# Six pairs in seven products: buffers for turned blocks, issues held back for free buffers, and an order laid out with one server for all DMAs

## The chip, the cores and the metric

The kernel runs on one core of a Trainium2 chip. The time of a run is the device time in microseconds (us) of that core, for one execution of the whole program. The number compared is the median over runs. The core has five engines that run their own instruction streams in order: TensorE (PE), VectorE (DVE), ScalarE (ACT), GpSimd (POOL) and SyncE (SP), which here issues nearly all transfers. Transfers are carried out by 16 DMA engines.

## The reference

Two decoder layers work on 256 tokens of width 1024, all in float32. Each layer is a half-step feed-forward block (SwiGLU), a mixer, and a second half-step feed-forward block:

```python
def swiglu(h, w_gate, w_up, w_down):
    return (jax.nn.silu(h @ w_gate) * (h @ w_up)) @ w_down

for layer in range(2):
    x = x + 0.5 * swiglu(rms_norm(x, ffn1_norm[layer]), ffn1_w_gate[layer], ffn1_w_up[layer], ffn1_w_down[layer])
    h = rms_norm(x, mix_norm[layer])
    ...   # layer 0: mLSTM beside cross-attention to 256 memory tokens; layer 1: dilated attention beside it
    x = x + mix
    x = x + 0.5 * swiglu(rms_norm(x, ffn2_norm[layer]), ffn2_w_gate[layer], ffn2_w_up[layer], ffn2_w_down[layer])
    ...   # after layer 0: keys and values for layer 1 are projected from x
```

The hidden width of the feed-forward blocks is 2816. The four of them hold most of the work, and the change lies in them. They are called (layer, which) below: (0,1), (0,2), (1,1), (1,2).

## The kernel before

**Products.** A float32 number is split into a rounded part `hi` (a cast on ACT) and a remainder `lo` (a subtraction on DVE), both in the fast format fp32r, and a product takes three matmuls: hi by lo, hi by hi, lo by hi (`mm3`). Weights come from HBM as tiles `raw` of 128x1024 (half a megabyte) through a ring of six buffers and are split into a ring of eight `hi`/`lo` pairs. So each weight tile is one transfer, one ACT operation, one DVE operation, and then 12 or 24 matmuls of 512 columns for the two tiles of 128 tokens.

**A feed-forward stage.** The hidden width is cut into 11 blocks of 256. For a block `b`, step `gb` (function `gu`) makes gate and up products in one bank of PSUM, `gups`, 24 matmuls for each of the two token tiles; step `db` (function `dn`) multiplies the activated block by its rows of the down weights into the accumulators `acc`, 12 matmuls per token tile. Between them stands the activation: ACT computes `sil`, DVE multiplies it to `h`, which frees the PSUM bank, and the block has to be turned, so that the hidden width lies on the partitions. Turning goes over DRAM: DVE writes both tiles' 32x32 transposes into a buffer `hb` (`hidden_blocks`, L1056), SP writes it out (`hd<-hb`) and reads it back in another order (`ht<-hd`), and ACT and DVE split the result into `hhb` and `hlb` for the down products (`placed`, L1066).

**Pairs in seven products.** Some neighbouring blocks are done as a pair with seven products in place of eight, after Strassen and Winograd: step `25` is product 2 of the pair that begins at block 5, 12 matmuls. Stages (0,1) and (1,1) have one pair (blocks 5 and 6), (0,2) and (1,2) have two (5 and 6, 7 and 8). For a pair the weights are four quarters in parts `pa`, `pb`, `pc`. Sums of them are made partly by transfers that add to what is in the buffer (issued by POOL, `accum_op`), partly by DVE (`remade`). A pair needs 14 `lo` operations and 6 such sums on DVE.

**What sets the order.** The order of the steps of a stage is written out by hand in the table `PLANS` (L49). `p` in it prepares weights of the next mixer. Everything beside the matmuls (splits, activations, turning, transfers) is emitted by chains of small steps. While the kernel is built, a planner (`_Model`, L251) keeps a clock for each engine and the time at which each buffer becomes ready or free by its cost table; at each point the chain that is ready first is emitted next (`until`). Since every engine runs its stream in order, the planner's numbers decide what stands behind what on the chip. A transfer is charged to SP's clock at 360 bytes per ns and lands 2.0 us after that; an adding transfer costs twice as much and lands 3.0 us after. `part_ready` (L605) decides from SP's clock when the next part of a pair may be loaded. All vector, scalar and transfer instructions are recorded by one helper and so bear one line, L369; all matmuls are L787, transposes on PE L794.

**Buffers on the way of a turned block.** There are two `hb`, four slots `hd` in DRAM and one `ht`. A chain takes its buffer, and emits the instruction that fills it, as soon as its turn comes, whether or not the planner thinks that the buffer is free by then:

```python
blocks[b] = fp.tile([P, 4, 2, 2, 32], F32, tag="hb", bufs=2 if pairs else 1, name="hb")
...
d = self.dram.tile([P, 512], F32, tag="hd", bufs=4, name="hd")
...
ht = fp.tile([P, 4, P], F32, tag="ht", bufs=1, name="ht")
```

On the chip the instruction then waits at the head of its engine's queue until the buffer's last reader is done.

Of the kernel before, what the change touches and what calls it, by code (L numbers as in the profile page):

```python
# [40 lines left out]
def turned(layer, which, b):  # L41
# [24 lines left out]
SOON = 8  # L66
TWICE = ((0, 1), (0, 2), (1, 2))
# [183 lines left out]
class _Model:  # L251
# [10 lines left out]
    def __init__(self):  # L262
        self.clock = {"scalar": 0.6, "vector": 0.6, "gpsimd": 0.6, "tensor": 0.6, "sync": 1.6}
        self.marks = {}
        self.slots = {}
        self.banks = set()
        self.table = None
        self.latest = 0.0
        self.window, self.columns, self.fast = 0, 0.0, False
# [79 lines left out]
    def adding(self, cost, outs, ins):  # L349

        start = max([self.clock["sync"]] + [self.ready(a, True, "sync") for a in outs])
        self.clock["sync"] += cost
        end = start + cost + 3.0
# [5 lines left out]
class _Engine:  # L359
# [5 lines left out]
    def __getattr__(self, method):  # L365
        call, model, name = getattr(self.engine, method), self.model, self.name

        def traced(out, *args, **kw):
# [8 lines left out]
            if name == "sync" or name == "gpsimd" and method == "dma_start":  # L377
                cost = max(n * out.partition_size() * 4 / 360e3, 0.06)
                if kw.get("accum_op") is None:
                    model.run("sync", cost, outs, ins, 2.0)  # L380
                else:
                    model.adding(2 * cost, outs, ins)
# [51 lines left out]
class _Kernel:  # L434
# [138 lines left out]

    def leave(self, pool, n=1):
# [30 lines left out]
    def part_ready(self):  # L605
# [9 lines left out]
        if not all(c is not None and c.done for c in chains):  # L615
            return False
        return self.index[("st",) + self.pairs[p] + (m, k)] <= self.next + SOON or \
            self.model.clock["sync"] < self.now + LEAD
# [395 lines left out]
    def ffn_in(self, layer, which, after, memory, fp):  # L1014
# [7 lines left out]
        pending = set()  # L1022
# [33 lines left out]
        def hidden_blocks(b, t):  # L1056
            def steps(ps):
                h = self.work.tile([P, FB], F32, tag="ta", bufs=4, name="h")
                yield from activated(ps, t, h)
                if b not in blocks:  # L1060
                    blocks[b] = fp.tile([P, 4, 2, 2, 32], F32, tag="hb", bufs=2 if pairs else 1, name="hb")
# [4 lines left out]
        def placed(b, before):  # L1066
            yield from self.wait(*before)
            hb = blocks.pop(b)
            d = self.dram.tile([P, 512], F32, tag="hd", bufs=4, name="hd")
            nc.sync.dma_start(d, hb.rearrange("p j c t e -> p (j c t e)"))  # L1070
            yield
            ht = fp.tile([P, 4, P], F32, tag="ht", bufs=1, name="ht")
# [6 lines left out]
                                  ht.rearrange("p i (c e) -> p i c e", c=4))  # L1079
            for t in range(2):  # L1080
# [943 lines left out]
```

## Time and profile before

| what | value |
|---|---|
| median of 3 runs | 1009.35 us (1008.54 to 1010.49) |
| the profiled execution's own time | 1005.82 us |
| span in its trace, from the first to the last instruction | 1003.9 us |
| mean granted clock of TensorE | 0.991 |
| HBM read, written | 206.28 MB, 17.85 MB |
| queue of SP's transfers | 81816 packets, 60.3% of the DMA engines' span |
| queue of POOL's transfers, the adding ones | 3456 packets, 7.0% |

The trace is of one execution, and its instructions are named by line, engine, operation and tile. A row of the chain of waits gives a start, a length, and what stood there on the path that ended last. A row by stage gives the busy time of each engine in a window. A row of waits gives who waited, for whom, the sum, the count and the longest, in us. The stages of the program in this execution, read from the tile names, lie at: (0,1) from 25 to 202 us, the first mixer with the memory's projections to 321, (0,2) to 513, keys and values for layer 1 to 545, (1,1) to 743, the second mixer to 815, (1,2) to the end. "hi", "lo", "h", "hhb" and the like are the tiles above; an arrow points from what is read to what is written, from right to left.

### The profile page before, as it was taken

What the parts mean: (1) busy time and instruction counts of PE and PEld (TensorE: products, weight loads), DVE (VectorE), ACT (ScalarE), POOL (GpSimd) and SP (SyncE); (2) the same over time, 40 slices, a digit from 0 to 9 for tenths busy, and PEclk for the clock granted to TensorE, in tenths of its full rate; (3) what the DMA queues carried; (4) which work ended last, traced back from release to release, by engine and by line L of the source; (5) the groups of instructions that cost most, each with busy time, mean ns of one, the idle gap of its engine ahead of it and who ended that gap; (6) DMA issues with size and microseconds to landing.
All of it is one profiled execution on the core that took longest, in us unless ns stands there. A gap on an engine that the chain in (4) does not pass through costs nothing.

```text
span 1003.9 us, 13192 instructions
## 1 busy us (share of the span) xinstructions
PE 974.9 (97%) x4607; PEld 804.8 (80%) x4607; DVE 773.3 (77%) x1133; ACT 591.1 (59%) x935; POOL 72.1 (7%) x102
## 2 busy tenths in 40 slices
PE   9999999999999999989999999899999999899998
PEld 7777888899898878868778888788887788787777
DVE  6979876669976789879576787987566878896972
ACT  7776555577755565555476565656565674564641
POOL 0031000010010010000012001100011000100000
PEclk9999999999999999989999999999999999999999
DMA  9899688555455769854655799378457265998271
GB/s 361 330 316 299 240 274 341 169 171 194 137 167 191 237 186 297 300 136 170 228 190 169 264 312 306 84 257 280 162 202 288 112 229 191 259 293 255 73 251 42
DMA packets 85481, 224.99 MB, mean 224 GB/s; under 512 B 8172, under 2 KB 29608, under 8 KB 85416
## 3 DMA queue, kind: packets, MB, share of 16 engines
q1 hardware_dynamic: 81816, 211.54, 60.3%
q0 software_dynamic: 3456, 12.58, 7.0%
q8 instruction: 36, 0.59, 0.2%
q14 instruction: 29, 0.24, 0.1%
q10 hardware_dynamic: 144, 0.04, 0.0%
HBM read 206.28 MB, written 17.85 MB: 223 GB/s over the span
## 4 chain that ended last, share of the span: by engine, by line
PE 61%; DMA 16%; DVE 13%; issue 5%; ACT 4%; POOL 1%; SPq 1%; DVEq 0%; ACTq 0%; POOLq 0%
PE gups L787 25%; PE acc L787 17%; PE aps L787 6%; DVE lo L369 6%; DMA ht<-hd 5%; DMA hd<-hb 5%; PE oacc L787 4%; PE kvps L787 3%; DMA pb<-in_wts 2%; DMA raw<-in_wts 2%; ACT hi L369 2%; PE bqps L787 2%; PE tps L794 1%; DVE h L369 1%; DVE hb L369 1%
## 5 line engine op out<-in xcount | busy, mean ns | idle before, releaser
L369 DVE TENSOR_TENSOR lo<-raw,hi 128x1024 fp32r<-128x1024 f32 (+2 forms) x239 | 271.9, 1159 | 58.6 <-ACT hi L369 56.9
L369 ACT CAST hi<-raw 128x1024 fp32r<-128x1024 f32 (+2 forms) x239 | 233.0, 1003 | 66.6 <-DMA raw<-in_wts 26.2
L787 PE MATMUL gups<-lo,xh 128*128 128x512 f32 x552 | 214.2, 391 | 0.0
L787 PE MATMUL gups<-hi,xh 128*128 128x512 f32 x552 | 214.1, 390 | 0.0
L787 PE MATMUL gups<-hi,xl 128*128 128x512 f32 x552 | 214.0, 390 | 0.0
L787 PE MATMUL acc<-lo,hhb 128*128 128x512 f32 x304 | 120.4, 396 | 2.9 <-ACT hhb L369 2.2
L787 PEld LDWEIGHTS gups<-hi,xh 128*128 128x128 f32 x552 | 103.8, 188 | 22.1 <-ACT hi L369 0.8
L787 PEld LDWEIGHTS gups<-hi,xl 128*128 128x128 f32 x552 | 103.9, 188 | 21.7
L787 PEld LDWEIGHTS gups<-lo,xh 128*128 128x128 f32 x552 | 104.0, 188 | 21.4
L787 PE MATMUL acc<-hi,hlb 128*128 128x512 f32 x304 | 119.3, 393 | 0.0
L787 PE MATMUL acc<-hi,hhb 128*128 128x512 f32 x304 | 118.9, 391 | 0.0
L369 DVE SCALAR_TENSOR_TENSOR lo<-raw,gains,hi 128x512 fp32r<-128x512 f32 x128 | 88.9, 745 | 12.3 <-ACT hi L369 12.1
L369 ACT ACTIVATE hi<-raw,gains 128x512 fp32r<-128x512 f32 x128 | 84.0, 717 | 12.4 <-PE acc L787 4.6
L369 ACT ACTIVATE sil<-gups,rstd 128x256 f32<-128x256 f32 x76 | 35.9, 472 | 69.2 <-PE gups L787 56.0
L787 PEld LDWEIGHTS acc<-lo,hhb 128*128 128x128 f32 x304 | 57.5, 189 | 15.5 <-ACT hhb L369 3.1
L787 PEld LDWEIGHTS acc<-hi,hlb 128*128 128x128 f32 x304 | 57.3, 189 | 12.9 <-DVE hlb L369 0.9
L787 PEld LDWEIGHTS acc<-hi,hhb 128*128 128x128 f32 x304 | 57.4, 189 | 11.4
L787 PE MATMUL gups<-lo,th 128*128 128x512 f32 x128 | 52.9, 413 | 12.5 <-DVE h L369 12.2
L369 ACT CAST hhb<-ht 128x512 fp32r<-128x512 f32 x38 | 23.6, 621 | 69.2 <-DMA ht<-hd 69.2
L369 DVE SCALAR_TENSOR_TENSOR h<-gups,rstd,sil 128x256 f32<-128x256 f32 x76 | 36.3, 478 | 26.6 <-ACT sil L369 26.5
L369 ACT CAST hi<-pb 128x1024 fp32r<-128x1024 f32 x36 | 37.4, 1050 | 26.9 <-DMA pb<-in_wts 19.6
L787 PE MATMUL gups<-hi,th 128*128 128x512 f32 x128 | 51.8, 405 | 0.0
(231 smaller groups left out, 1592.9 us busy)
## 6 DMA issues: line engine op xcount, KB each, us to landing
raw<-in_wts SPq DMA_DIRECT2D x262, 512.0 KB, 5.3
raw<-in_wts SPq DMA_DIRECT2D x32, 384.0 KB, 3.6
hd<-hb SPq DMA_DIRECT2D x38, 256.0 KB, 5.4
ht<-hd SPq DMA_DIRECT2D x38, 256.0 KB, 4.2
pa<-in_wts SPq DMA_DIRECT2D x12, 512.0 KB, 6.7
pb<-in_wts SPq DMA_DIRECT2D x12, 512.0 KB, 4.5
pc<-in_wts SPq DMA_DIRECT2D x12, 512.0 KB, 6.4
pc<-in_wts POOLq DMA_DIRECT2D x12, 512.0 KB, 8.6
```

The lines of the kernel that those rows point to most:

```text
L369: call(out, *args, **kw)
L787: self.pe.matmul(out, lhsT=lhsT, rhs=rhs, start=start, stop=stop, skip_group_check=more)
L794: self.pe.transpose(out, in_, ident)
```

## The change

Four things change, and no instruction is added or taken away on any engine: the same operations stand in another order, with other buffers.

1. Buffers: three `hb` in place of two, two `ht` in place of one, eight slots `hd` in place of four.
2. A chain that needs an `hb` or an `ht` first waits, in the planner's time, until the oldest buffer is free (`vacant`), and no more blocks may be under way than there are buffers (`held_by`). Only then it takes the buffer and emits the instruction.
3. The planner's cost of transfers. One clock, `wire`, stands for all DMA engines together: each transfer, whoever issues it, begins when the one before it is through, takes a time from its size and the length of its contiguous pieces, 2.06 times as much if it adds, and lands 1.03 us later. The issuing engine's own clock is charged 0.34 us (0.9 for an adding transfer), and it waits there for the transfer's inputs and its buffer. `part_ready` goes by `wire`.
4. `PLANS` has a new order for all four stages. In (0,2) and (1,2) `d0` and `d1` stand further ahead, `d3` before `75`, and `d4` before `77`; in (1,1) the memory's step (tied to `g4`) before `g3`, `25` and `55` ahead of `d2`, `d3` and `d7` earlier; in (0,1) a `p` moves from behind `15` to before `35`.

```diff
 PLANS = {
-    (0, 1): "g0 g1 g2 g4 p d0 g3 25 55 d1 d2 45 d4 35 "
-            "d3 p 15 p 65 75 g7 p g8 d6 g9 p d5 d7",
-    (0, 2): "g0 g1 g2 g3 25 55 d0 d1 d2 45 35 15 65 75 "
-            "d3 g9 g4 27 57 d5 47 37 17 67 77 d4 d9 d6",
-    (1, 1): "g0 g1 g2 d0 g3 d1 g4 d2 25 55 45 "
-            "35 d3 15 65 d4 75 g7 g8 d5 d6 g9 d7",
-    (1, 2): "g0 g1 g2 g3 25 55 d0 d1 d2 45 35 15 65 75 "
-            "d3 g9 g4 27 57 d5 47 37 17 67 77 d4 d9 d6",
+    (0, 1): "g0 g1 g2 g4 p d0 g3 25 55 d1 d2 45 d4 p "
+            "35 d3 p 15 65 75 g7 p g8 d6 g9 p d5 d7",
+    (0, 2): "g0 g2 g1 d0 g3 d1 25 55 d2 45 35 15 65 d3 "
+            "75 g9 g4 27 57 47 d5 37 17 67 d4 77 d9 d6",
+    (1, 1): "g0 g1 g2 d0 g4 g3 d1 25 55 d2 45 "
+            "d3 35 15 65 d4 75 g7 g8 d5 d7 d6 g9",
+    (1, 2): "g0 g1 g2 d0 d1 g3 25 55 d2 45 35 15 65 d3 "
+            "75 g9 g4 27 57 d5 47 37 17 67 d4 77 d9 d6",
 }
...
+HB, HT = 3, 2
...
-    def adding(self, cost, outs, ins):
-        start = max([self.clock["sync"]] + [self.ready(a, True, "sync") for a in outs])
-        self.clock["sync"] += cost
-        end = start + cost + 3.0
+    def transfer(self, engine, outs, ins, adding=False):
+        size = outs[0].free_size() * outs[0].partition_size()
+        piece = min(self.piece(outs[0]), self.piece(ins[0]), 1024)
+        cost = size / piece * (8.2 + 0.147 * piece) / 16e3
+        at = max([self.ready(a, False, "sync") for a in ins] +
+                 [self.ready(a, True, "sync") for a in outs] + [self.clock[engine]])
+        self.clock[engine] = at + (0.9 if adding else 0.34)
+        begin = max(self.wire, at + 0.3)
+        if adding:
+            cost *= 2.06
+        self.wire = begin + cost
+        end = max(begin, at + 1.9 if adding else 0.0) + cost + 1.03
...
-                cost = max(n * out.partition_size() * 4 / 360e3, 0.06)
-                if kw.get("accum_op") is None:
-                    model.run("sync", cost, outs, ins, 2.0)
-                else:
-                    model.adding(2 * cost, outs, ins)
+                model.transfer(name, outs, ins, kw.get("accum_op") is not None)
...
+    def vacant(self, pool, tag, bufs):
+        waited = 0.0
+        while True:
+            t = self.model.free((id(pool), tag), bufs)
+            if t <= max(self.now, waited):
+                return
+            waited = t
+            self.model.latest = max(self.model.latest, t)
+            yield
...
-            self.model.clock["sync"] < self.now + LEAD
+            self.model.wire < self.now + LEAD
...
+        def held_by(count, most):
+            while count[0] >= most:
+                yield 0.05
+            count[0] += 1
...
                 if b not in blocks:
-                    blocks[b] = fp.tile([P, 4, 2, 2, 32], F32, tag="hb", bufs=2 if pairs else 1, name="hb")
+                    yield from self.vacant(fp, "hb", HB)
+                    yield from held_by(turning, HB)
+                    blocks[b] = fp.tile([P, 4, 2, 2, 32], F32, tag="hb", bufs=HB, name="hb")
...
-            d = self.dram.tile([P, 512], F32, tag="hd", bufs=4, name="hd")
+            d = self.dram.tile([P, 512], F32, tag="hd", bufs=8, name="hd")
             nc.sync.dma_start(d, hb.rearrange("p j c t e -> p (j c t e)"))
+            turning[0] -= 1
             yield
-            ht = fp.tile([P, 4, P], F32, tag="ht", bufs=1, name="ht")
+            yield from self.vacant(fp, "ht", HT)
+            yield from held_by(placing, HT)
+            ht = fp.tile([P, 4, P], F32, tag="ht", bufs=HT, name="ht")
```

**How instructions move.** SP's queue in (0,2), between the two pairs: the weights `raw189` to `raw191` belong to steps `g9` and `g4`, `hd` and `ht` are the way of a turned block. Before:

```order
L369 DMA hd_4145<-hb_4089 128x512
L369 DMA hd_4168<-hb_4065 128x512
L369 DMA raw189_4177<-in_wts 128x1024
L369 DMA raw190_4189<-in_wts 128x1024
L369 DMA raw191_4201<-in_wts 128x1024
L369 DMA ht_4235<-hd_4145 128x4x128
L369 DMA ht_4240<-hd_4168 128x4x128
L369 DMA hd_4264<-hb_4220 128x512
L369 DMA ht_4321<-hd_4264 128x4x128
```

The same place after the change:

```order
L389 DMA hd_4143<-hb_4070 128x512
L389 DMA pc2_4157<-in_wts 128x1024
L389 DMA raw186_4164<-in_wts 128x1024
L389 DMA raw187_4167<-in_wts 128x1024
L389 DMA raw190_4192<-in_wts 128x1024
L389 DMA hd_4198<-hb_4057 128x512
L389 DMA raw191_4201<-in_wts 128x1024
L389 DMA ht_4223<-hd_4143 128x4x128
L389 DMA hd_4273<-hb_4226 128x512
L389 DMA ht_4299<-hd_4198 128x4x128
L389 DMA raw192_4337<-in_wts 128x1024
L389 DMA ht_4351<-hd_4273 128x4x128
```

The two writes and the two reads of a pair's blocks stood in twos, and now stand apart: the second read is behind the write of a third block, `hd_4273`.

DVE at the same place. `hlb` splits a turned block, `h` frees the PSUM bank of a product, `lo` splits weights. Before:

```order
L369 TENSOR_TENSOR pa2_3971<-pa2_3971,pb2_3990 128x1024
L369 TENSOR_TENSOR hlb_4286<-ht_4235,hhb_4285 128x4x4x32
L369 SCALAR_TENSOR_TENSOR h_4293<-gups_4245,rstd_3292,sil_4294 128x256
L369 TENSOR_TENSOR hlb_4308<-ht_4240,hhb_4307 128x4x4x32
L369 STREAM_TRANSPOSE hb_4326<-h_4293 128x2x4x32
L369 TENSOR_TENSOR lo176_4315<-raw176_4133,hi176_4314 128x1024
L369 TENSOR_TENSOR lo177_4324<-raw177_4136,hi177_4323 128x1024
L369 SCALAR_TENSOR_TENSOR h_4343<-gups_4296,rstd_3357,sil_4344 128x256
```

And after, where the last `hb` of the third block and an `h` and `hb` of the fourth stand just ahead of the first row:

```order
L389 TENSOR_TENSOR lo176_4307<-pc0_4072,hi176_4306 128x1024
L389 TENSOR_TENSOR lo177_4317<-pc2_4157,hi177_4316 128x1024
L389 TENSOR_TENSOR hlb_4320<-ht_4223,hhb_4319 128x4x4x32
L389 TENSOR_TENSOR lo178_4330<-raw178_4130,hi178_4329 128x1024
L389 TENSOR_TENSOR pc0_4072<-pc0_4072,pa0_3958 128x1024
L389 SCALAR_TENSOR_TENSOR h_4339<-gups_4291,rstd_3357,sil_4340 128x256
L389 TENSOR_TENSOR lo179_4360<-raw179_4136,hi179_4359 128x1024
L389 TENSOR_TENSOR lo180_4363<-pb0_4014,hi180_4362 128x1024
L389 TENSOR_TENSOR pb0_4014<-pb0_4014,pa0_3958 128x1024
L389 STREAM_TRANSPOSE hb_4301<-h_4339 128x2x4x32
L389 TENSOR_TENSOR pc2_4157<-pc2_4157,pa2_3960 128x1024
L389 TENSOR_TENSOR hlb_4384<-ht_4299,hhb_4383 128x4x4x32
```

Two `hlb` with one `h` between them have become two `hlb` with eight other operations between them.

DVE in (1,1), at the memory's keys `kn` (two chains of scaling, `hss` and scaling again, each behind ACT's squares `sq`). Before:

```order
L369 TENSOR_TENSOR hlb_5975<-ht_5888,hhb_5974 128x4x4x32
L369 TENSOR_TENSOR lo248_5995<-pa_5626,hi248_5994 128x1024
L369 TENSOR_TENSOR lo249_5998<-pa_5628,hi249_5997 128x1024
L369 TENSOR_SCALAR kn_6016<-mkvps_5951,memr0_90 128x256
L369 TENSOR_TENSOR lo250_6008<-pb0_5759,hi250_6007 128x1024
L369 TENSOR_TENSOR pa_5626<-pa_5626,pb0_5759 128x1024
L369 TENSOR_REDUCE hss_6032<-sq_6018 128x4
L369 TENSOR_SCALAR kn_6044<-mkvps_5977,memr1_91 128x256
L369 TENSOR_TENSOR hlb_6042<-ht_6014,hhb_6041 128x4x4x32
L369 TENSOR_REDUCE hss_6066<-sq_6046 128x4
```

After:

```order
L389 TENSOR_SCALAR kn_5891<-mkvps_5813,memr0_90 128x256
L389 TENSOR_TENSOR lo244_5880<-raw244_5785,hi244_5879 128x1024
L389 TENSOR_REDUCE hss_5908<-sq_5893 128x4
L389 TENSOR_SCALAR kn_5918<-mkvps_5842,memr1_91 128x256
L389 TENSOR_REDUCE hss_5938<-sq_5920 128x4
L389 TENSOR_TENSOR lo245_5927<-raw245_5799,hi245_5926 128x1024
L389 TENSOR_TENSOR lo246_5933<-pa_5594,hi246_5932 128x1024
L389 TENSOR_TENSOR lo247_5951<-pa_5596,hi247_5950 128x1024
L389 TENSOR_TENSOR kn_5891<-kn_5891,rp_r_5911 128x256
L389 TENSOR_TENSOR kn_5918<-kn_5918,rp_r_5941 128x256
```

The `hlb` of a turned block no longer stands inside the two chains, and the pair's parts (`pa`) come after them.

More of the change, by code (lines that the diff above doesn't have):

```diff
@@ L262, in __init__ @@
     def __init__(self):
-        self.clock = {"scalar": 0.6, "vector": 0.6, "gpsimd": 0.6, "tensor": 0.6, "sync": 1.6}
+        self.clock = {"scalar": 0.6, "vector": 0.6, "gpsimd": 0.6, "tensor": 0.6, "sync": 2.1}
         self.marks = {}
@@ L267, in __init__ @@
         self.table = None
-        self.latest = 0.0
+        self.latest, self.wire = 0.0, 0.0
         self.window, self.columns, self.fast = 0, 0.0, False
@@ L347, in run, with piece @@
         self.latest = max(self.latest, end)
-    def adding(self, cost, outs, ins):
-        start = max([self.clock["sync"]] + [self.ready(a, True, "sync") for a in outs])
-        self.clock["sync"] += cost
-        end = start + cost + 3.0
+    @staticmethod
+    def piece(ap):
+        run = 1
+        for step, n in reversed(ap.ap[1:]):
+            if step != run:
+                break
+            run *= n
+        return run
+    def transfer(self, engine, outs, ins, adding=False):
[10 more added lines that the diff above has]
+        end = max(begin, at + 1.9 if adding else 0.0) + cost + 1.03
+        for a in ins:
+            self.mark(a, end, False, "sync")
         for a in outs:
@@ L1021, in ffn_in @@
         pairs = (layer, which) in PLANS
-        pending = set()
+        pending, turning, placing = set(), [0], [0]
+        def held_by(count, most):
+            while count[0] >= most:
+                yield 0.05
+            count[0] += 1
         def room(*key):
@@ L1079, in placed @@
                                   ht.rearrange("p i (c e) -> p i c e", c=4))
+            placing[0] -= 1
             for t in range(2):
```

## The prediction

> **What bounds the kernel now.** I read the page first, then the busy time by stage, then who made TensorE (PE) wait in each stage, and the chain of waits for what a wait costs afterwards.
>
> ```profile
> PE 974.9 (97%) x4607; PEld 804.8 (80%) x4607; DVE 773.3 (77%) x1133; ACT 591.1 (59%) x935; POOL 72.1 (7%) x102
> ```
>
> PE is the bound: 97% busy, and the program holds the same instructions before and after. So the change can win only what PE loses to waits. The stages (window, its length, then busy time and instructions of PE, its weight loads, VectorE (DVE), ScalarE (ACT) and GpSimd (POOL), the granted clock, the share of the DMA engines, GB/s):
>
> ```profile
> 202.00:321.00 119.00, 117.66 (x702) 107.49 (x702) 93.49 (x192) 78.17 (x158) 11.18 (x24) 1.00 0.52 170
> 321.00:513.00 192.00, 183.34 (x795) 149.31 (x794) 151.51 (x190) 106.71 (x147) 9.10 (x13) 0.97 0.67 216
> ...
> 545.00:743.00 198.00, 195.14 (x863) 161.16 (x862) 151.66 (x218) 118.62 (x181) 8.64 (x10) 0.99 0.70 226
> 743.00:815.00 72.00, 69.38 (x442) 53.90 (x441) 51.27 (x106) 42.79 (x96) 9.69 (x12) 1.00 0.57 211
> 815.00:1003.90 188.90, 178.96 (x788) 146.32 (x785) 144.96 (x180) 96.31 (x126) 7.90 (x10) 0.99 0.64 201
> ...
> 25.00:202.00 177.00, 174.68 (x787) 143.62 (x786) 141.96 (x182) 108.99 (x157) 14.03 (x15) 1.00 0.82 282
> ```
>
> The losses sit in three feed-forward stages: 192 − 183.3 = 8.7 us in (0,2), 9.9 us in (1,2) (some 3 of it the tail after the last product), 2.9 us in (1,1). Only these stages show a clock under 1.00. Who PE waited for, in (0,2), then (1,1), then (1,2):
>
> ```profile
> PE gups L787 <- DVE h L369: 5.9, 2, 4.6
> PE acc L787 <- ACT hhb L369: 1.8, 1, 1.8
> PE acc L787 <- DVE lo L369: 0.7, 1, 0.7
> ...
> PE tpk L794 <- DVE kn L369: 2.9, 1, 2.9
> ...
> PE gups L787 <- DVE h L369: 6.4, 3, 3.2
> PE acc L787 <- ACT hhb L369: 0.4, 1, 0.4
> ```
>
> And what followed these waits, from the chain (start, length, what, count):
>
> ```profile
> 438.72 5.44 PE gups L787 x12
> ...
> 449.63 10.89 PE gups L787 x48
> ...
> 489.43 2.51 PE acc L787 x6
> ...
> 636.76 9.07 PE gups L787 x36
> ...
> 865.64 3.04 PE gups L787 x12
> ...
> 931.97 4.61 PE gups L787 x12
> ```
>
> 48 matmuls in 10.89 us are 0.227 us each, 12 are 2.72. The 12 behind the 4.6 us wait took 5.44: half clock, 2.7 us more. By the same count the other rows lost 1.2, 0.9, 0.3 and 1.9 us. The Trainium skill ("TensorE: Matmul & The Clock Gate", section "HAM oscillation") puts the danger at PE gaps over about 3.4 us; the trace differs, since a gap of 1.8 us was followed by half clock and one of 3.2 by hardly any. By that rule only the first clock loss would be there, and the prizes below would be 4.3 us smaller; the sum goes by the rows.
>
> So the prizes are: **A** (0,2), start of the second pair, 4.6 + 2.7 = 7.3. **B** (0,2), end, 1.8 + 1.2 = 3.0. **C** (0,2), start of the first pair, (5.9 − 4.6) + 0.7 = 2.0. **D** (1,1), 2.9 + 0.9 = 3.8. **E** (1,2), first pair, 3.2 + 0.3 = 3.5. **F** (1,2), second pair, (6.4 − 3.2) + 1.9 = 5.1. Together 24.7 us: the most that can be won here.
>
> **Part by part.** *Two `ht` buffers and held-back issues.* Around A:
>
> ```profile
> 420.56 9.16 SPq L369 DMA_DIRECT2D ht<-hd  x2
> ...
> 434.31 0.62 ACT L369 CAST hhb<-ht 128x512 fp32r<-128x512 f32 x1 [7.54 <-DMA ht<-hd]
> ...
> 434.96 0.69 DVE L369 TENSOR_TENSOR hlb<-ht,hhb 128x512 fp32r<-128x512 f32 x1 [5.25 <-ACT hhb L369]
> ...
> 438.18 0.48 DVE L369 SCALAR_TENSOR_TENSOR h<-gups,rstd,sil 128x256 f32<-128x256 f32 x1
> ...
> 429.35 4.94 DMA ht<-hd
> ...
> L369 DVE TENSOR_TENSOR lo<-raw,hi 128x1024 fp32r<-128x1024 f32 x196 | 234.1, 1216 | 52.3 <-ACT hi L369 50.8
> ```
>
> Both reads are next to each other on SP's queue, but the second leaves only at 429.35, when `hlb` of the first has emptied the one buffer. DVE, in order, stands 5.25 us at the second `hlb`; behind it is the `h` that frees PE's bank. With a second buffer the read no longer waits for that `hlb`. In the new order it stands behind the write of a third block (`hd_4273` in the rows shown with the change), but after that block's last `hb` DVE has eight operations of 128x1024, one `hlb` and four small ones, 8 x 1.22 + 0.69 + 4 x 0.48 or about 12 us, before the second `hlb`, more than twice what the read took (4.94). Bounds for A: all 7.3 gone, or nothing (if adds delay the read). I take 5.3 of A and of F, the same place one layer later, 3.6 of 5.1, leaving a wait under 2 us at each.
>
> *B and the end of (1,2)* have the same serial pair of reads:
>
> ```profile
> 473.14 7.14 DMA ht<-hd
> ...
> 481.68 4.47 DMA ht<-hd
> ```
>
> The second could land some 5 us earlier. But the plan also moves `d4` in front of `77`: between product 7 of blocks 7 and 8 and the first down product of block 7 stand three groups of 24 matmuls (`d9 d6` and half of `g10`) instead of four, 16.3 us instead of 21.8. Gain and loss nearly cancel. For B I take 1.5 won (bounds 3.0 won, 3.0 lost); at the end of (1,2), **G**, where PE now waits 0.4 us, 1.5 lost (0 to 5).
>
> *C and E*: `d0` and `d1` now stand before `25`. In (0,2) `d1` (24 matmuls, 5.4 us) separates the last `g3` product from `25`, so the `h` that frees the bank and the `lo` have that much more time than the waits of 1.3 and 0.7. In (1,2) `g3` still touches `25`, but `d0 d1` in front leave DVE work done sooner. I take 1.5 of C's 2.0 and 2.0 of E's 3.5 (bounds: all, none).
>
> *D*: the memory's products move up (`g4` before `g3`).
>
> ```profile
> 615.63 9.27 DMA hd<-hb
> ...
> 627.90 0.62 ACT L369 CAST hhb<-ht 128x512 fp32r<-128x512 f32 x1 [5.12 <-DMA ht<-hd]
> ...
> 629.30 0.48 DVE L369 TENSOR_SCALAR kn<-mkvps,memr 128x256 f32<-128x256 f32 x1 [3.40 <-ACT sq L369]
> ```
>
> ACT stood 5.12 us at `hhb`, with the `sq` behind it for which DVE's `kn`, and then PE, waited. In the new order no `hlb` stands between the two `kn` chains. I take 3.3 of 3.8.
>
> *The other tight places*, **H**: `d1` of (0,2) and of (1,2) follow their block's last product by 72 matmuls (16.3 us), `d9` of (1,1) by 60 (13.6 instead of 19.1).
>
> ```profile
> 697.51 10.88 PE gups L787 x48
> ...
> 720.62 0.62 ACT L369 CAST hhb<-ht 128x512 fp32r<-128x512 f32 x1 [0.84 <-DMA ht<-hd]
> ```
>
> Block 9's products ended at 708.4; its `hhb` was ready 12.8 us later, 0.8 inside the new room. I take 1.0 lost (0 to 6). **J**: the new DMA times shift rows in the mixers too, whose stages idle 1.3 and 2.6 us, and in (0,1), 2.3: 1.0 lost (3 either way). The third `hb` buffer, the eight `hd` slots and the 0.3 to 0.4 us that a further SP issue takes add no instruction; costed at nothing, hidden under PE.
>
> **The sum:** 5.3 + 1.5 + 1.5 + 3.3 + 2.0 + 3.6 = 17.2 won, 1.5 + 1.0 + 1.0 = 3.5 lost: 13.7. The profiled execution took 1005.8 us (1003.9 of span, the end of the last window above, and 1.9 around it), so 992.1; it was 3.5 below the median of the timed runs, 1009.35. On that scale the forecast is **995.5 us**.
>
> **Rivals.** *1, the adds share the wire.* The planner now serves all transfers one after another. But in the window 866.5 to 878.2, with four adds under way (software queue q0, SP's queue q1):
>
> ```profile
> q0 software_dynamic: 405, 1.46, 65.1%
> q1 hardware_dynamic: 513, 1.64, 38.9%
> ...
> hd<-hb SPq DMA_DIRECT2D x1, 256.0 KB, 11.6
> ht<-hd SPq DMA_DIRECT2D x1, 256.0 KB, 6.2
> ```
>
> Both queues moved at once, and a turned block needed 11.6 + 6.2 = 17.8 us. In both (x,2) stages the block turned beside the first pair's adds now has less DVE work between its last `hb` and its `hlb`: in (0,2) ten operations of 128x1024 and two of half that size instead of nineteen and one; in (1,2) fewer still. 10 x 1.22 and, at half the time, 2 x 0.6 are 13.4 us: DVE would stand 4.4. A pair is 14 `lo` and 6 sums, 24.4 us of DVE against 84 matmuls, 19.1 of PE, so nothing there catches it up. Twice 4.4 lost on top of the forecast: 1004. The Trainium skill ("DMA: Bandwidth & Descriptors", section "Queues, rings and completion order") says that each DMA engine goes round its queues packet by packet, which these two rows agree with; by that rule this rival is the likelier the more adds are under way. Against it: the planner also counts an add dear, so it may place `hlb` late enough.
>
> *2, slower: the rooms of 16.3 us are too short.* At the end of (1,2):
>
> ```profile
> 963.93 0.42 SPq L369 DMA_DIRECT2D hd<-hb  x1
> ...
> 959.85 6.04 DMA hd<-hb
> ...
> 965.90 6.84 DMA ht<-hd
> ```
>
> The last product ended near 955.6 (13.6 us after 942.0), the write of block 7 left 8.3 us later; with 6.0 and 6.8 for the trips and 0.6 for `hhb` that is 21.7, 5.4 over the room, and with half clock after it some 7.5 a place. At three of the five places with 13.6 to 16.3 us that is 22.5, against 16.2 won elsewhere (13.7 plus the 2.5 of G and H): 1015.7. It decides once the trip exceeds 16.3 us at three places. Against it: `ht` took 2.9 there as the second read, and d0 and d1 start with quieter queues.
>
> *3, the stops only move.* DVE has no reserve inside a pair, and the new order's hold-ups fall elsewhere in the same runs: of the 17.2 us 3 to 7 stay won, less 3.5: about 1007.
>
> **How the numbers follow.** Forecast 0.58, rival 1 0.18, rival 2 0.11, rival 3 0.13. A measurement here tells 0.2%, 2 us, from no change. Faster: all of the forecast's case, 0.16 of rival 1, 0.07 of rival 3: 0.81. Same: 0.02 and 0.04: 0.06. Slower: rival 2 and 0.02 of rival 3: 0.13. The range runs from 984 (all 24.7 us won) to 1010, which takes in rivals 1 and 3; the forecast's own is 988 to 1002.
>
> **What would show it.** Right: the waits of PE for `h` in (0,2) and (1,2) fall from 12.3 us together to under 5, the wait for `kn` in (1,1) is gone, the clock in (0,2) is 0.99 or more, and no second read waits over 2 us for an `hlb`. Rival 1: DVE stands over 3 us at an `hlb` inside a first pair. Rival 2: PE waits for `hhb` at the ends of stages grow from 2.2 us to over 8. The forecast is wrong if PE idle in the three stages together stays over 17 us, or if the mixers' idle grows by more than 3.

## The result, and the profile after

The change made the kernel slower: 1024.39 us median of 4 runs (1022.39 to 1027.61) against 1008.94 us before, a ratio of 1.0153 with a 95% interval of 1.0123 to 1.0184. The forecast was 995.5 us, and the range ended at 1010. The profiled execution took 1022.39 us, with a span of 1020.7 and a mean granted clock of 0.985.

The page of the changed kernel, engines first:

```profile
PE 978.6 (96%) x4607; PEld 806.7 (79%) x4607; DVE 773.6 (76%) x1133; ACT 590.5 (58%) x935; POOL 70.3 (7%) x102
```

The work is what it was; DVE is busy 0.3 us longer and ACT 0.6 us shorter. PE is busy 3.7 us longer, with a granted clock of 0.985 against 0.991, and idle 13 us longer. Where, by stage (window, its length, then busy time and instructions of PE, its weight loads, DVE, ACT and POOL, the granted clock, the share of the DMA engines, GB/s), with every stage reaching to the first matmul of the next. The changed kernel:

```profile
0.00:204.40 204.40, 198.08 (x861) 160.52 (x862) 156.35 (x209) 126.26 (x192) 12.56 (x23) 0.98 0.82 284
204.40:323.90 119.50, 119.50 (x724) 109.44 (x722) 95.32 (x195) 80.16 (x164) 10.59 (x25) 1.00 0.53 176
323.90:517.50 193.60, 182.28 (x787) 147.95 (x785) 149.87 (x189) 104.75 (x144) 8.82 (x12) 0.96 0.66 212
...
553.80:754.50 200.70, 193.02 (x846) 157.59 (x845) 148.71 (x213) 114.52 (x175) 8.41 (x10) 0.99 0.68 222
754.50:830.60 76.10, 70.18 (x450) 55.05 (x448) 52.40 (x108) 43.84 (x97) 11.41 (x12) 1.00 0.53 193
830.60:1020.70 190.10, 179.23 (x784) 147.26 (x782) 143.94 (x180) 96.17 (x126) 7.92 (x10) 0.98 0.63 202
```

The same cut of the kernel before:

```profile
0.00:200.00 200.00, 196.44 (x862) 159.20 (x863) 155.50 (x209) 125.92 (x192) 15.96 (x23) 1.00 0.83 291
200.00:321.40 121.40, 120.06 (x723) 109.83 (x722) 95.55 (x195) 80.57 (x164) 11.55 (x25) 1.00 0.53 172
321.40:512.10 190.70, 182.04 (x788) 148.25 (x787) 150.38 (x189) 105.41 (x145) 8.85 (x12) 0.97 0.67 216
...
548.30:742.30 194.00, 191.14 (x845) 157.94 (x844) 147.86 (x213) 114.64 (x174) 8.64 (x10) 0.99 0.70 229
742.30:815.40 73.10, 70.48 (x448) 54.73 (x448) 52.37 (x108) 43.89 (x97) 9.69 (x12) 1.00 0.57 210
815.40:1003.90 188.50, 178.56 (x785) 146.00 (x783) 144.57 (x180) 95.91 (x126) 7.90 (x10) 0.99 0.63 201
```

(0,1) is 4.4 us longer, the first mixer 1.9 shorter, (0,2) 2.9 longer, (1,1) 6.7, the second mixer 3.0, (1,2) 1.6; with 0.1 for the keys and values that is the 16.8 us between the spans. No stage that was to gain gained. Who PE waited for in the changed kernel:

```profile
PE gups L814 <- DVE h L389: 17.0, 5, 6.9
PE tph L821 <- DVE h L389: 4.5, 3, 3.3
PE tpq L821 <- DVE qn L389: 3.3, 1, 3.3
PE mkvps L814 <- DVE h L389: 3.0, 2, 1.8
...
PE gups L814 <- DVE lo L389: 1.9, 1, 1.9
PE acc L814 <- ACT hhb L389: 1.4, 1, 1.4
```

The waits of `gups` for `h` in (0,2) and (1,2), which were to fall from 12.3 us together to under 5, are 14.8 there (7.2 and 7.6), and 17.0 in all; the longest is the one of place A, 6.9 where it was 4.6. PE's idle time in the three stages that were to gain is 29.9 us together; over 17 was the prediction's sign of being wrong. Two stops are new, of 3.3 us each: `h` at 22 us, in a stretch of (0,1) whose order was not changed, and `qn` in the second mixer.

**Place A.** DVE and ACT at the start of the second pair of (0,2):

```profile
437.11 1.23 DVE L389 TENSOR_TENSOR lo<-pc,hi 128x1024 fp32r<-128x1024 f32 x1 [2.24 <-ACT hi L389]
442.47 0.69 DVE L389 TENSOR_TENSOR hlb<-ht,hhb 128x512 fp32r<-128x512 f32 x1 [4.14 <-ACT hhb L389]
```

```profile
441.82 0.62 ACT L389 CAST hhb<-ht 128x512 fp32r<-128x512 f32 x1 [4.75 <-DMA ht<-hd]
```

DVE stands again, but at the first `hlb` of the place, not the second. The buffer is free; the read is late. What the DMA engines did around it, between 417 and 442 us (GB/s in 40 slices, then packets, MB and the share of the engines of each queue; q0 is that of the adds):

```profile
GB/s 210 243 177 262 236 282 308 269 367 390 380 403 433 410 429 419 426 413 423 403 393 419 403 322 284 220 213 200 211 249 239 232 252 232 229 211 215 204 178 59
...
q1 hardware_dynamic: 2555, 5.28, 56.7%
q0 software_dynamic: 576, 2.10, 43.4%
```

And what was issued from 413 to 427 us (count, size, median us from issue to landing):

```profile
raw<-in_wts SPq DMA_DIRECT2D x8, 512.0 KB, 9.3
...
pc<-in_wts SPq DMA_DIRECT2D x1, 512.0 KB
ht<-hd SPq DMA_DIRECT2D x1, 256.0 KB, 15.2
```

The two queues together fill all engines (56.7% and 43.4%). Nine weight transfers were issued in the 13 us ahead of the read, 9.3 us each in the median from issue to landing, so the later ones were still under way when it was issued; and three adds were issued behind it, from 428.27 to 431.64 us (a row of SP's queue, then two of POOL's):

```profile
426.57 0.38 SPq L389 DMA_DIRECT2D ht<-hd  x1
...
428.27 0.86 POOL L389 DMA_DIRECT2D pc<-in_wts  x1 [12.71 <-DMA pc<-in_wts]
...
431.64 0.86 POOL L389 DMA_DIRECT2D pb<-in_wts  x1 [1.62 <-issue]
```

The read lands 15.2 us after its issue. A read that has the wire to itself, in the same execution at 342 us, takes 2.6:

```profile
ht<-hd SPq DMA_DIRECT2D x1, 256.0 KB, 2.6
```

The same kind of window before the change (420 to 434 us), where the prediction's 4.94 us for the read came from, has a wire that lies idle for some 4 us, from 424 to 428:

```profile
GB/s 386 410 433 457 386 410 394 332 331 192 95 38 16 22 20 0 0 0 0 0 0 0 0 0 152 70 47 140 140 222 187 187 199 181 287 332 299 238 231 263
```

SP issued no weight transfer between 418 and 437 us. The read itself, from 429.35 us on, was not alone: two adds, issued at 426.98 and 429.25, ran beside it. So 4.94 us is the time of a read beside adds with no weights in its own queue.

**The second mixer.** ACT in the changed kernel, and below it in the kernel before:

```profile
785.84 1.05 ACT L389 CAST hi<-raw 128x1024 fp32r<-128x1024 f32 x1 [2.89 <-DMA raw<-in_wts]
786.80 0.55 ACT L389 ACTIVATE mp<-ms,nm,rqb 128x256 f32<-128x256 f32 x1
```

```profile
771.76 0.56 ACT L369 ACTIVATE mp<-ms,nm,rqb 128x256 f32<-128x256 f32 x1 [0.95 <-DVE nm L369]
...
773.81 1.06 ACT L369 CAST hi<-raw 128x1024 fp32r<-128x1024 f32 x1 [0.48 <-DMA raw<-in_wts]
```

A cast of weights has moved ahead of `mp`, and stands 2.9 us for its transfer; `qn`, for which PE waits, comes behind it. At 22 us it is a cast too, but not the wait of a single one. ACT in the changed kernel, and below it in the kernel before:

```profile
18.99 1.05 ACT L389 CAST hi<-raw 128x1024 fp32r<-128x1024 f32 x1 [2.04 <-DMA raw<-in_wts]
...
21.62 1.05 ACT L389 CAST hi<-raw 128x1024 fp32r<-128x1024 f32 x1 [0.31 <-DMA raw<-in_wts]
```

```profile
18.58 1.05 ACT L369 CAST hi<-raw 128x1024 fp32r<-128x1024 f32 x1 [2.03 <-DMA raw<-in_wts]
```

The stop of 2.0 us stands in both. The changed kernel has one cast more, the one at 21.62, ahead of the work that leads to `h`, which begins at 25.53 us and not at 23.78; and PE comes to the transpose of `h` sooner, its last product ahead of it beginning at 22.41 us and not at 24.26.

### The profile page after: what moved, and what is told of

Read it like the earlier page. It is cut to its first block, busy times and chain, and to the rows that moved or that the text cites. A ratio compares the mean times of both kernels' runs of the same rounds, so it can differ in the third digit from the quotient of the medians.

```text
span 1020.7 us, 13205 instructions
## 1 busy us (share of the span) xinstructions
PE 978.6 (96%) x4607; PEld 806.7 (79%) x4607; DVE 773.6 (76%) x1133; ACT 590.5 (58%) x935; POOL 70.3 (7%) x102
## 3 DMA queue, kind: packets, MB, share of 16 engines
q0 software_dynamic: 3456, 12.58, 6.6%
## 5 line engine op out<-in xcount | busy, mean ns | idle before, releaser
L814 PE MATMUL gups<-lo,xh 128*128 128x512 f32 x552 | 216.9, 396 | 4.3 <-DVE h L389 2.4
L389 DVE TENSOR_TENSOR hlb<-ht,hhb 128x512 fp32r<-128x512 f32 x38 | 26.1, 687 | 55.4 <-ACT hhb L389 55.4
```

The source lines that it names most:

```text
L389: call(out, *args, **kw)
L814: self.pe.matmul(out, lhsT=lhsT, rhs=rhs, start=start, stop=stop, skip_group_check=more)
```

## The experiments

All kernels ran beside the kernel before on the same chip. There are 4 to 10 runs of each. Runs of one kernel scatter by up to 1.6% (the kernel before: 1003.88 to 1008.96 in 13 runs on one chip, 996.53 to 1012.54 in 15 on another), so the ratios to before are compared, with 95% intervals:

| kernel | orders | planner's costs | median us | ratio to before |
|---|---|---|---|---|
| the change | new | new | 1024.39 | 1.0153 (1.0123 to 1.0184) |
| buffers_only (no issues held back) | old | old | 993.67 | 0.9873 (0.9838 to 0.9907) |
| held_back | old | old | 994.31 | 0.9899 (0.9830 to 0.9969) |
| old_costs | new | old | 1014.02 | 1.0081 (1.0052 to 1.0109) |
| old_plans | old | new | 1019.47 | 1.0126 (1.0083 to 1.0170) |
| late_landing | new | new, later landing | 1007.40 | 1.0010 (0.9994 to 1.0027) |
| late_old_plans | old | new, later landing | 997.70 | 0.9913 (0.9883 to 0.9942) |
| plain_adds | new | new; adds only copy | 1005.92 | 1.0005 (0.9978 to 1.0033) |
| plans_plain | new | old; adds only copy | 993.54 | 0.9887 (0.9842 to 0.9931) |
| late_plain | new | later landing; adds only copy | 998.50 | 0.9940 (0.9915 to 0.9965) |
| buffers_plain | old | old; adds only copy | 990.76 | 0.9883 (0.9819 to 0.9946) |
| ht_only (two `ht`) | old | old | 999.55 | 0.9935 (0.9903 to 0.9967) |
| hb_ht (two `ht`, three `hb`) | old | old | 992.06 | 0.9882 (0.9850 to 0.9913) |
| early_d4 (on buffers_only) | `d4 77` | old | 996.65 | 0.9911 (0.9875 to 0.9946) |
| d_early (on buffers_only) | first steps new | old | 994.72 | 0.9893 (0.9856 to 0.9931) |
| d3_early (on buffers_only) | `d3 75` | old | 999.21 | 0.9946 (0.9912 to 0.9980) |
| keys_earlier (on buffers_only) | `g4 g3` in (1,1) | old | 994.92 | 0.9911 (0.9881 to 0.9941) |

### Which part of the change costs

The kernel before with the buffer numbers alone:

```diff
-... tag="hb", bufs=2 if pairs else 1, ...   tag="hd", bufs=4, ...   tag="ht", bufs=1, ...
+... tag="hb", bufs=3, ...                   tag="hd", bufs=8, ...   tag="ht", bufs=2, ...
```

> The kernel before with three hb, two ht and eight hd, nothing else. If a second buffer removes the wait at the second hlb, as the prediction said of its place A: PE's wait for h in (0,2) falls from 5.9 to about 1 us and the time to some 1000 us (7.3 and up to 5 us less). If the stop goes elsewhere: 1006 to 1011 us.

With held-back issues as well (the change with the orders and the costs of before):

```diff
+                    yield from self.vacant(fp, "hb", HB)
+                    yield from held_by(turning, HB)
...
+            yield from self.vacant(fp, "ht", HT)
+            yield from held_by(placing, HT)
```

> The kernel before with the buffers and the held-back issues, but the orders and the transfer costs of before. If holding back costs nothing: 990 to 997 us, as with the buffers alone (993.7), and the 20 us between that kernel and the one with the new orders and old costs (1014.0) belong to the new orders. If holding back is what costs: 1005 to 1014 us.

The change with the old orders, and the change with the old costs:

```diff
 (old_plans)
-    (0, 2): "g0 g2 g1 d0 g3 d1 25 55 d2 45 35 15 65 d3 "
-            "75 g9 g4 27 57 47 d5 37 17 67 d4 77 d9 d6",
+    (0, 2): "g0 g1 g2 g3 25 55 d0 d1 d2 45 35 15 65 75 "
+            "d3 g9 g4 27 57 d5 47 37 17 67 77 d4 d9 d6",
 ...
 (old_costs)
-                model.transfer(name, outs, ins, kw.get("accum_op") is not None)
+                cost = max(n * out.partition_size() * 4 / 360e3, 0.06)
+                if kw.get("accum_op") is None:
+                    model.run("sync", cost, outs, ins, 2.0)
+                else:
+                    model.adding(2 * cost, outs, ins)
 ...
-            self.model.wire < self.now + LEAD
+            self.model.clock["sync"] < self.now + LEAD
```

(In old_costs the clock of the transfers also starts at 1.6 us again, as before; the change starts it at 2.1.)

> The changed kernel with the four orders of before in PLANS; buffers, held-back issues and the new transfer costs stay. Theory P (the new orders cost the 15 us, by groups set nearer to what they wait for): about 1000 us, with the stops of (1,1) near the 3 us of before; the first stop in (0,1), at 22 us, does not depend on the order of the stage and stays. Theory M (the new transfer costs let the planner put casts ahead of transfers that land later than it thinks): 1016 to 1026 us, with the stops at 22 us and in the second mixer still there and a long read in (0,2).

> The changed kernel with the old costs of transfers in the planner (360 bytes per ns on SP's clock, landing 2.0 us later, parts released by SP's clock); buffers, held-back issues and the new orders stay. Theory M (the new transfer costs are what costs): 998 to 1008 us, the stop at 22 us gone, the second mixer back from 76 to 73 us. Theory P (the orders): 1018 to 1026 us, with (1,1) still some 200 us long.

Measured: the buffers win 1.3%, and holding issues back takes nothing of it that can be told (0.9899 against 0.9873). On top of that the new orders cost 1.8% (1.0081 less 0.9899) and the new costs 2.3% (1.0126 less 0.9899). So neither theory is right alone: both lose, and together they lose 2.5%, less than the sum; why is not shown. By stage, in the one execution profiled of each, the new orders with the old costs lose against held_back 8.4 us in (0,2), 7.5 in (1,2), 5.7 in (0,1) and nothing in (1,1). Waits of PE in the kernel with the buffers alone:

```profile
PE tpk L794 <- DVE kn L369: 5.3, 3, 2.9
PE gups L787 <- DVE h L369: 4.9, 2, 2.7
...
PE acc L787 <- ACT hhb L369: 1.2, 1, 1.2
```

The waits for `h` are 4.9 us where they were 12.2, and none is left at the start of a second pair. (0,2) takes 182.2 us and (1,2) 181.9, 8.5 and 6.6 less than before:

```profile
323.30:505.50 182.20, 178.88 (x787) 146.61 (x785) 150.41 (x189) 105.62 (x144) 8.82 (x12) 0.99 0.70 226
...
809.50:991.40 181.90, 175.97 (x784) 145.00 (x782) 144.22 (x180) 96.37 (x126) 7.88 (x10) 1.00 0.65 208
```

### The landing time in the planner

In the new costs a transfer of 512 KB that has the wire to itself takes 1.27 us there and lands 2.6 us after its issue. In the trace of the changed kernel such a transfer, issued at 295.88 us when nothing else had moved for 3.9 us, took 3.4; the old costs (1.46 at 360 bytes per ns, and 2.0) put it at 3.5:

```profile
raw<-in_wts SPq DMA_DIRECT2D x1, 512.0 KB, 3.4
```

One number altered in the changed kernel, and then the same with the old orders:

```diff
-        end = max(begin, at + 1.9 if adding else 0.0) + cost + 1.03
+        end = max(begin, at + 1.9 if adding else 0.0) + cost + (1.03 if adding else 2.0)
```

> The changed kernel with one number altered: the planner lets a transfer that does not add land 2.0 us after the wire is through with it, not 1.03. In the trace a lone transfer of 512 KB takes 3.4 to 3.5 us from its issue to its landing, the planner's figure is 2.6. Theory M1 (it is the too early landing that puts casts ahead of late transfers): the stops at 22 us and in the second mixer go and 8 us or more are won: 1005 to 1016 us. Theory M2 (it is the one server, which does not know how adds and reads share the engines): 1018 to 1028 us. Theory P: 1018 to 1028 us.

> The changed kernel with the four orders of before and with transfers that land 2.0 us after the wire in the planner. Theory M1 (the new costs lose by the too early landing alone): 992 to 998 us, as with the old costs (994.3). Theory M2 (one server without sharing loses beside that): 1004 to 1014 us, with stops at the starts of pairs.

With the new orders the time falls to 1.0010 of before, 1.4% less than the change; with the old orders from 1.0126 to 0.9913, 2.1%, to where the old costs stand (0.9899). Theory M1 holds for the time: what the new costs lose, they lose by a landing that comes too early. The stage that lost most, (1,1), shows it best: from its first product to the first matmul of the next stage it takes 200.7 us in the change and 201.0 with the old orders and the new costs (old_plans), but 193.5 to 198.3 in the ten kernels with adds and the old costs, and 195.1 and 196.7 with the later landing (one execution of each). So its 6.7 us are for the most part not the work of its order. In the second mixer (76.1 us, here 72.9) the cast of weights is behind `mp` again:

```profile
774.11 0.55 ACT L389 ACTIVATE mp<-ms,nm,rqb 128x256 f32<-128x256 f32 x1
...
774.83 1.05 ACT L389 CAST hi<-raw 128x1024 fp32r<-128x1024 f32 x1
```

The one server in itself costs nothing that can be told (0.9913 against 0.9899 with the old orders), and with the new orders it does better than the old costs (1.0010 against 1.0081). The stop at 22 us became shorter (2.0 us) but did not go, against the expectation: the further cast is still ahead there, at 21.48 us.

### The adding transfers

Four of the kernels above, with every instruction in its place, but with POOL's transfers told to copy, so that the sums of the pairs' parts are left out; the planner still counts them as adding:

```diff
-            call(out, *args, **kw)
+            call(out, *args, **{k: v for k, v in kw.items() if k != "accum_op"})
```

> The changed kernel, every instruction in the same place, but POOL's adding transfers only copy (the sums of a pair's parts are left out, so that part of the computation is missing). Theory R1 (the first rival: adds share the engines with the reads of turned blocks): in the second pair of (0,2) the read that took 15.2 us from issue to landing takes under 11, the stop of 7.1 us falls under 3, that of 4.8 us in (1,2) too, and the time is 1008 to 1014 us. Theory Q (the read stands behind the nine weight transfers of its own queue): the read still takes 13 us or more, the stops stay within 1.5 us, 1018 to 1024 us.

> The kernel with the new orders, the buffers, the held-back issues and the old costs (1014.0 us), every instruction in the same place, but POOL's transfers only copy (the sums of a pair's parts are left out). If the new orders lose by the adds, as the whole change did (15 us less without them): 998 to 1004 us. If they lose by rooms that are too short for an idle wire as well: 1008 to 1014 us.

> Control: the kernel before with the three buffer numbers, every instruction in the same place, POOL's transfers only copy (the sums are left out). If the adds cost only where a read of a turned block falls beside them: 988 to 993 us, at most 5 us less than with adds (993.7). If copying in place of adding saves everywhere, whatever the order: 975 to 985 us.

> The changed kernel with transfers that land 2.0 us after the wire in the planner, and with POOL's adding transfers that only copy (the sums of a pair's parts are left out). If too early landing and adds beside reads are the whole loss: 990 to 997 us, where the buffers alone are. If there is a third cause, or if rooms that are too short remain: 1000 to 1007 us.

The change falls from 1.0153 to 1.0005. At place A the read that took 15.2 us takes 9.0, with as many weight transfers ahead of it (issued from 409.5 to 423 us), copies issued behind it in place of adds, and the `hlb` goes through without a stop; PE's waits for `h` in (0,2) are 0.2 us in place of 7.2, and in (1,2) 3.2 in place of 7.6:

```profile
raw<-in_wts SPq DMA_DIRECT2D x8, 512.0 KB, 8.2
...
pc<-in_wts SPq DMA_DIRECT2D x1, 512.0 KB
ht<-hd SPq DMA_DIRECT2D x1, 256.0 KB, 9.0
```

```profile
433.21 0.68 DVE L389 TENSOR_TENSOR hlb<-ht,hhb 128x512 fp32r<-128x512 f32 x1
```

Theory R1 holds (a read under 11 us, stops under 3, and a time below the 1008 us expected); theory Q does not, though its part is real, since 9.0 us is still over three times what a lone read takes. Without adds the new orders lose nothing: with the old costs they stand at 0.9887, against 0.9883 for the old orders (the control). The control says that copying saves next to nothing by itself, 0.9883 against 0.9873 with adds. So the 1.8% of the new orders are lost through the adds. At the places looked at, it is a turned block's write or read that falls beside them; a copy also lands sooner itself (7.6 us after its issue for the one at 411.56 us, where the add in its place took 10.0), and what part of the gain that is, is not shown. With the later landing the longest stop left is 6.8 us for `hhb`, in the first pair of (1,2), which is where the first rival looked for it; with copies as well (late_plain) the waits for `hhb` in that stage are 1.4 us.

With both causes taken away the change stands at 0.9940, between the expectations: 0.6% over the control, with intervals that overlap. In the one execution profiled (0,1) is the stage that stays long, 204.4 us against 197.9 in the control, with a wait of 2.5 us for `h` at its start. But five kernels that build this stage alike (buffers_only and the four of the next part) have it between 197.7 and 201.9 us, so one execution says little.

### The orders one by one

On the kernel with the buffers alone and the old costs:

```diff
 (early_d4, both stages with two pairs)
-            "d3 g9 g4 27 57 d5 47 37 17 67 77 d4 d9 d6",
+            "d3 g9 g4 27 57 d5 47 37 17 67 d4 77 d9 d6",
 (d_early)
-    (0, 2): "g0 g1 g2 g3 25 55 d0 d1 d2 45 35 15 65 75 "
+    (0, 2): "g0 g2 g1 d0 g3 d1 25 55 d2 45 35 15 65 75 "
-    (1, 2): "g0 g1 g2 g3 25 55 d0 d1 d2 45 35 15 65 75 "
+    (1, 2): "g0 g1 g2 d0 d1 g3 25 55 d2 45 35 15 65 75 "
 (d3_early, both)
-  ... 15 65 75 "
-            "d3 g9 ...
+  ... 15 65 d3 "
+            "75 g9 ...
 (keys_earlier)
-    (1, 1): "g0 g1 g2 d0 g3 d1 g4 d2 25 55 45 "
+    (1, 1): "g0 g1 g2 d0 g4 g3 d1 d2 25 55 45 "
```

> The kernel before with the three buffer numbers, and d4 put ahead of 77 in (0,2) and (1,2). Second rival (the room of 16.3 us between product 7 and the first down product is too short): with the buffers alone PE waited 1.4 us for hhb at the end of (0,2) and had 3 us to spare in (1,2); 5.4 us less room makes waits of 5 to 7 and 2 to 4 us, with some clock: 1000 to 1006 us. If the way of the block gets shorter as well: 992 to 997 us.

> The kernel before with the three buffer numbers, and in (0,2) and (1,2) the blocks' first steps in the new order (d0 and d1 ahead of 25, g2 ahead of g1 in (0,2)); the rest of the orders stays. The prediction's terms C and E: the waits of 2.3 us at 370 and 2.9 us at 856 fall, 988 to 992 us. If the block's weights and reads now fall together with the pair's adds (first rival): 997 to 1006 us, with a read of over 10 us in the first pair.

> The kernel before with the three buffer numbers, and d3 put ahead of 75 in (0,2) and (1,2), nothing else. Theory W (d3's weights are then asked for while the second pair's adds and the first pair's blocks are on the way, so the reads land late and DVE stands at hlb): a read of over 8 us and a stop of 2 us or more at the start of the second pairs, 998 to 1006 us. Without that: 991 to 996 us.

> The kernel before with the three buffer numbers, and in (1,1) g4, with the memory's step behind it, ahead of g3 and d1 (g0 g1 g2 d0 g4 g3 d1 d2 25); no other order is changed. Step D of the prediction: the wait of 3.1 us for kn at 626 falls under 1 us, and the time is 3 us lower: 988 to 992 us. If a stop takes its place (the memory's products waiting for h, as with the new orders, 3.7 us): 992 to 997 us.

None wins. `d3` ahead of `75` costs most, 0.7%, and the intervals just do not overlap: PE waits 4.2 us for `h` at the start of the second pair of (0,2), where the buffers alone left none. The reads there took 5.8 us, not over 8 as expected; it is the writes, 11.7 us beside adds and weight transfers, that came late (issued from 409.5 to 424 us):

```profile
hd<-hb SPq DMA_DIRECT2D x2, 256.0 KB, 11.7
ht<-hd SPq DMA_DIRECT2D x2, 256.0 KB, 5.8
```

`d4` ahead of `77` costs 0.4% within overlapping intervals; the wait for `hhb` at the end of (0,2) grew from 1.2 to 3.0 us. The first steps' order moves stops about and leaves the time where it was: in (0,2) the wait for `h` became waits for `lo` and for the sums `g`:

```profile
PE gups L787 <- DVE g L369: 3.2, 2, 1.6
PE gups L787 <- DVE lo L369: 2.9, 2, 2.1
```

And the memory's keys earlier in (1,1), step D, do the same: 1.8 us for `kn` in place of 2.9, and a new wait of 2.0 ahead of it (one execution, of 1000.3 us against a median of 994.9).

```profile
PE mkvps L787 <- DVE h L369: 2.0, 1, 2.0
PE tpk L794 <- DVE kn L369: 1.8, 2, 1.2
```

### Which buffer

The kernel before with two `ht` alone, and with two `ht` and three `hb`:

```diff
 (ht_only, hb_ht)
-            ht = fp.tile([P, 4, P], F32, tag="ht", bufs=1, name="ht")
+            ht = fp.tile([P, 4, P], F32, tag="ht", bufs=2, name="ht")
 (hb_ht)
-                    blocks[b] = fp.tile([P, 4, 2, 2, 32], F32, tag="hb", bufs=2 if pairs else 1, name="hb")
+                    blocks[b] = fp.tile([P, 4, 2, 2, 32], F32, tag="hb", bufs=3, name="hb")
```

> The kernel before with two ht and nothing else. The prediction put the gain of place A on the second ht and counted the third hb and the eight hd at nothing: by that 992 to 997 us, as with all three buffers (993.7). If the third hb or the hd slots carry the gain: 1003 to 1009 us.

> The kernel before with three hb and two ht, and four hd as before. If the third hb carries what the second ht alone does not give: 991 to 996 us. If the eight hd slots do: 998 to 1002 us. The prediction counted both at nothing, which would make this and the run with two ht alone the same.

The second `ht` gives 0.65%, the third `hb` a further 0.5% (0.9882), though the two intervals overlap; the four further `hd` slots give nothing more (0.9873). buffers_only and hb_ht are the fastest complete kernels here, 1.2 to 1.3% under the kernel before.

## Why the prediction was wrong

**What bounds the kernel, and the prizes**: right. The start of the second pairs could be won in full: with the buffers alone the stops of A and F are gone, and the 12.5 us won on that chip (1006.16 to 993.67) compare with the 10.4 that the prediction put on A, F and B.

**A and F, two `ht` and held-back issues**: the mechanism was right, and the third `hb`, counted at nothing, carried about half by the medians. In the changed kernel both places got no better: 6.9 us for 4.6 at A, 4.6 for 3.2 at F. The step that failed is "about 12 us, before the second `hlb`, more than twice what the read took (4.94)". It looked at the second `hlb` alone, as the place of the old stop, while the first was the late one (the second went through without a stop); and it took the duration of the read from a stretch in which two adds ran beside it but no weights stood in its own queue. The new order has nine weight transfers issued ahead of it and three adds behind, and the read took 15.2 us.

**Rival 1, the adds share the wire**: this was the mechanism, with a chance of 0.18. The price was too low, 8.8 us counted against the 15 that the copies give back (4.4 a place against stops of 6.9 and 4.6), and the place was another: it named the first pairs, and the trace of the change has the worst stops at the starts of the second, at A with weight transfers in the read's own queue as well. (At the first pairs its stop came out only with the later landing, 6.8 us in (1,2).) Its time, 1004, came from putting it on top of gains that were not there either. The argument against it ("the planner also counts an add dear") failed: the planner serves transfers one after another, so an add delays only what is issued after it, while in the trace the three adds were issued 1.7 to 5.1 us after the read, and with copies in their places (1.7 to 7.3 us after it) the read took 9.0 us and not 15.2. The rule of the Trainium skill that the prediction cited ("DMA: Bandwidth & Descriptors", section "Queues, rings and completion order") agrees with the copies: with half the time in the adds' queue the read in the other queue came 6 us sooner.

**J, "the new DMA times shift rows in the mixers too ... 1.0 lost (3 either way)"**: this term was mis-sized, and it hid a cause that no rival named. (0,1) lost 4.4 us, the second mixer 3.0, the first won 1.9: 5.5 lost together. And the new costs did not stop at these stages: in (1,1) the early landing took 4 to 6 us more. The new costs land a weight transfer 0.8 us too early (2.6 against 3.4); the planner then takes its cast for ready, and in the second mixer ACT, in order, is seen to stand at it. By the runs with the later landing that is 1.4% with the new orders, 2.1% with the old. Which instruction stands in (1,1) is not shown. The prediction named the new formula as a mere shift of rows; it did not set its landing against the trace. The same page of the Trainium skill (section "Anatomy of one DMA — SWDGE (gpsimd) path") puts a fixed part of about 2.0 us beside the time of the bytes, for transfers that GpSimd issues; the trace nearly agrees for SP's: 3.4 less the 1.27 that the planner counts for the bytes are 2.1 us. The planner's fixed part is 1.33.

**C and E**: counted at 1.5 and 2.0. In the changed kernel C's wait for `h` at the start of the first pair of (0,2) is gone, but 17 and 28 us further on, in the same pair, PE waits 1.9 and 0.9 us for `lo`; E's place still waits 3.0 for `h`. Alone, this order won nothing (0.9893 against 0.9873). The step "so much more time than the waits" treated DVE's work as movable; it stops at another operand instead. That was rival 3's idea, at the pairs' starts.

**D**: counted at 3.3. The wait for `kn` got 1.1 us shorter and `mkvps` waits 3.0 us for `h`; keys_earlier shows the same exchange without anything else changed. That (1,1) lost 6.7 us is for the most part the early landing, since the old orders lose as much there with the new costs (201.0 us).

**B, G, H and rival 2**: PE waited 1.4 us at the end of (0,2), not at all for `hhb` at the end of (1,2), and nowhere for `d1` or `d9`. The rooms were no trouble in the change: `d4` early costs some 4 us over two stages alone (0.4%, within overlapping intervals), and 7.5 a place was worked out from a trip with one `ht`.

**The sum** of what a change to the order of work may win was thus read from waits, one by one, as if each could be taken out with all else in its place. **What stays open**: the remainder of 0.6% with both causes gone, which the intervals do not hold firmly; the stop at 22 us, which outlived the later landing; and why the two losses do not add up (1.8% and 2.3% alone, 2.5% together).

## What to carry to other kernels

Take a transfer's duration from the state of the wire in which it will run, not from the one in which it ran: the same kind of read took 2.6 us alone, 4.9 beside two adds, 9.0 behind weights with copies beside it, and 15.2 behind weights with adds beside it. A planner's table must be set against the time from issue to landing: a landing that is 0.8 us too early put work of engines that run in order behind transfers that were not there yet, and cost 1.4 to 2.1% here. And where several changes come together, the plain one (a buffer more) is worth running alone first: here it was 1.3% faster than before, and the rest of the change lost twice that.

## What was not expected of the hardware

An adding transfer holds the engines about twice as long as a copy of the same bytes, which the planner's 2.06 already said; its cost shows in other transfers, which it did not say. The adds' queue in the changed kernel, and with copies in their place:

```profile
q0 software_dynamic: 3456, 12.58, 6.6%
```

```profile
q0 software_dynamic: 3456, 12.58, 3.6%
```

6.6% of 16 engines over 1020.7 us are 1078 us, 312 ns for each of 3456 packets; 3.6% over 1005.7 us are 579 us, 168 ns each. On all 16 engines together that is 67 us of a full wire in place of 36. The 31 us more cost the changed kernel 15 us of its time, where, at the places looked at, it waits for turned blocks, and cost the kernel with the buffers alone nothing that can be told (0.9873 with adds, 0.9883 without).
